# Dilated attention by residues modulo 4 in place of parities: 320 keys a query in place of 416, fp32 products on small array tiles

## The chip, the cores and the metric

The kernel runs on one core of a Trainium2 chip. A core has a matrix engine (TensorE, PE in the profile; its weight loads are listed as PEld), a vector engine (VectorE, DVE), a scalar engine (ScalarE, ACT), GpSimd (POOL) and SyncE (SP), which here only issues transfers. TensorE writes into PSUM, eight banks of 512 fp32 columns on 128 partitions. The metric is the device time of one execution in microseconds (us).

## The reference

One encoder layer on a stream of 512 positions and 1024 channels, fp32 throughout. A combined input projection gives the recurrent input, a gate, and q, k, v. The recurrent half is a gated linear recurrence in both directions. The other half is what the change touches: attention with 8 heads of 64 channels, with three windows for each query and a bias by relative position. Both halves are normed and go through an output projection of 1024 x 1024, and a two-layer MLP (1024 to 4096 to 1024) follows.

```python
DILATED_PATTERNS = ((128, 1), (512, 4), (2048, 16))
for window, dil in DILATED_PATTERNS:
    half = window // (2 * dil)
    offs = jnp.arange(-half, half + 1, dtype=jnp.int32) * dil
...
    logits = einsum(q, k[kpos]) * scale + bias        # NEG_INF where kpos is outside 0..S-1
    lse = logsumexp(logits); p = exp(logits - lse); outs.append(einsum(p, v[kpos]))
w = softmax(stack(lses))
o = sum(w * stack(outs))
```

So a query at position i needs every key with |j - i| up to 64, every fourth key (same residue modulo 4) with |j - i| up to 256, and every sixteenth key anywhere. A key that lies in two or three windows counts two or three times. Combining the windows by their denominators is the same as one softmax over all keys with the logarithm of that count added to the bias, and both kernels compute it so: one table of biases by relative position, with a large negative number where no window reaches.

## The kernel before, in words

**Stages.** The input projection comes first, in the order recurrent input, gate, v, then q and k for the first pair of heads. The attention stage follows, from about 94 to 176 us of the profiled execution. Then come the rest of the output projection, the MLP in two halves, and the final norm. Large products are made from splits: an operand is written as a rounded high part (ScalarE, line 247 for weights) and the remainder (VectorE, line 269), and a product is three matmuls (`mm3`, lines 312 to 314). The gates of the recurrence (`lru_gates`, PSUM name `pg`, line 528) are plain fp32 on tiles of 64 x 64 of the array. A plain fp32 matmul leaves two records in the trace.

**Attention before.** Heads go in four pairs p, one head of a pair on partitions 0 to 63 and the other on 64 to 127. Keys and queries are ordered by parity: even positions, then odd ones. For every pair there are four query tiles of 128, numbered u in the loop.

- `att_s` (line 806): scores, 128 queries x 416 keys, as three split products for each of two heads; a call makes two query tiles, so 12 matmuls. The 416 keys are the 256 of the query's own parity and 160 near ones of the other parity.
- `att_e`: VectorE adds the biases and finds the minimum (line 822); ScalarE takes the exponential and sums it (line 823).
- `att_t` (line 842): TensorE turns the weights in 128 x 128 blocks, six for each (p, u), into `pt`; ScalarE copies them out (line 845). `att_c` (line 851) turns the remaining 32 columns on VectorE.
- `att_av` (line 942): values, 24 matmuls of 64 output rows for a pair, plain fp32, the operand `vs` stationary. VectorE multiplies by the reciprocals of the sums (line 948), which come through a small round trip to DRAM (`att_z`, `att_zd`).
- `load_tw` (lines 476 and 478): biases for a head and a key offset, two transfers each from the table `nbd` in DRAM, 32 in all.
- `q_evac`, `k_evac`, `s_hi`, `s_lo` (lines 778, 784, 788): q and k are taken from PSUM, then split in a high and a low part; the first 256 columns of k are repeated behind the others by a transfer.

**The order around it.** The loop at lines 1139 to 1176 runs i = 0 to 4, u = 0 to 3. Step (i, u) issues the scores of pair i and the transposes of pair i - 1, and between them `fill` takes projection steps off a list: first the q and k projections of the later pairs, then the first half of the output projection (`wo_thunks`). The table `plan` puts the recurrence's leftovers and the splits at fixed places. Each engine works its own instructions in the order written out here. SP's transfers are in a fixed order too: weights, biases, and the round trip. PSUM is divided into four banks for projections (`pj`), two for scores and values (`gs`) and two for transposes (`et`). A weight block is read from DRAM (`wraw`), split (`whi`, `wlo`), and lasts for eight projection steps.

## Time and profile before

| what | value |
|---|---|
| median of 3 runs | 525.96 us (525.91 to 526.02) |
| span of the profiled execution | 524.0 us |
| TensorE busy | 517.3 us, 99% of the span, 3021 records |
| VectorE busy | 430.3 us, 82% |
| ScalarE busy | 351.9 us, 67% |
| chain that ended last | 96% TensorE |

The span runs from the first instruction to the last in one profiled execution; the time of a run also holds what lies around it. The views used below are: the page's totals of each engine; the chain of work that ended last, followed back from the last instruction; groups of instructions by line (busy time, mean and extremes of one in ns, when the first started and the last ended); and stretches, which give each engine's busy time in a window. A line such as `PE ps L806 x12` is twelve TensorE records that write to `ps`, issued by line 806 of the kernel.

### The profile page before, as it was taken

How to read it: one execution, taken by the hardware profiler on the slowest of the kernel's cores; microseconds unless marked ns; L12 is line 12 of the kernel's file. 1: busy time of each engine (PE TensorE's matmuls, PEld its weight loads, DVE VectorE, ACT ScalarE, POOL GpSimd, SP SyncE). 2: the span in 40 equal slices, each digit the busy share in tenths (PEclk: the TensorE clock that was granted, in tenths of full speed). 3: DMA queues.
4: the chain of work that ended last, by engine and by line, in shares of the span. 5: the costliest groups of instructions: out<-in, count | busy, mean ns of one | idle time of the engine just before them, and what ended most of it. 6: DMA issues, size and time to landing. Idle time of an engine off the chain costs nothing.

```text
span 524.0 us, 8211 instructions
## 1 busy us (share of the span) xinstructions
PE 517.3 (99%) x3021; PEld 444.0 (85%) x3021; DVE 430.3 (82%) x668; ACT 351.9 (67%) x568; POOL 65.8 (13%) x90
## 2 busy tenths in 40 slices
PE   9999999999999999999999999999999999999995
PEld 8867888778787788899999888889999999888884
DVE  6899986788886898898789987789766978986985
ACT  7579946667855848585578666565667577655664
POOL 0173000000000321001300311001101300140000
PEclk9999999999999999999999999999999999999999
DMA  8636545367696499847595899976977497799804
GB/s 288 213 98 198 160 155 180 91 182 206 185 286 218 102 194 275 326 129 196 136 225 144 217 273 275 309 268 161 295 235 194 116 226 208 154 286 256 201 1 161
DMA packets 40329, 105.15 MB, mean 201 GB/s; under 512 B 5056, under 2 KB 13376, under 8 KB 40288
## 3 DMA queue, kind: packets, MB, share of 16 engines
q1 hardware_dynamic: 32448, 78.10, 44.7%
q0 software_dynamic: 7696, 26.32, 27.1%
q8 instruction: 24, 0.39, 0.3%
q10 hardware_dynamic: 144, 0.20, 0.1%
q14 instruction: 17, 0.14, 0.1%
HBM read 95.59 MB, written 4.29 MB: 191 GB/s over the span
## 4 chain that ended last, share of the span: by engine, by line
PE 96%; issue 2%; DVE 1%; POOL 1%; DVEq 0%; ACT 0%; POOLq 0%; ACTq 0%
PE pu L313 10%; PE pu L312 10%; PE pu L314 10%; PE pd L312 10%; PE pd L313 10%; PE pd L314 10%; PE pqk L312 3%; PE pqk L314 3%; PE pqk L313 3%; PE pwo L312 2%; PE pt L842 2%; PE pwo L314 2%; PE pwo L313 2%; PE ps L806 2%; PE pav L942 2%
## 5 line engine op out<-in xcount | busy, mean ns | idle before, releaser
L269 DVE TENSOR_TENSOR wlo<-wraw,whi 128x1024 fp32r<-128x1024 f32 x71 | 86.6, 1221 | 23.1 <-ACT whi L247 22.9
L247 ACT ACTIVATE whi<-wraw 128x1024 fp32r<-128x1024 f32 x67 | 70.8, 1058 | 37.5 <-PE pd L314 18.2
L313 PE MATMUL pd<-wlo,ah 128*128 128x512 f32 (+1 forms) x195 | 75.2, 386 | 0.0
L312 PE MATMUL pd<-whi,ah 128*128 128x512 f32 (+1 forms) x195 | 75.2, 386 | 0.0
L314 PE MATMUL pd<-whi,al 128*128 128x512 f32 (+1 forms) x195 | 75.2, 386 | 0.0
L314 PE MATMUL pu<-hh,wlo 128*128 128x256 f32 x224 | 63.4, 283 | 0.0
L313 PE MATMUL pu<-hl,whi 128*128 128x256 f32 x224 | 63.4, 283 | 0.0
L312 PE MATMUL pu<-hh,whi 128*128 128x256 f32 x224 | 63.4, 283 | 0.0
L269 DVE TENSOR_TENSOR wlo<-tw,whi 128x1024 fp32r<-128x1024 f32 x37 | 45.2, 1221 | 18.1 <-ACT whi L247 18.1
L312 PE MATMUL pu<-h2h,whi 128*128 128x256 f32 (+1 forms) x200 | 60.1, 300 | 0.0
L313 PE MATMUL pu<-h2l,whi 128*128 128x256 f32 (+1 forms) x200 | 60.0, 300 | 0.0
L314 PE MATMUL pu<-h2h,wlo 128*128 128x256 f32 (+1 forms) x200 | 60.0, 300 | 0.0
L247 ACT ACTIVATE whi<-tw 128x1024 fp32r<-128x1024 f32 x38 | 40.1, 1059 | 26.3 <-PE pd L314 6.3
L247 ACT ACTIVATE whi<-ts 128x1024 fp32r<-128x1024 f32 x24 | 25.5, 1061 | 26.3 <-PE pd L314 18.3
L312 PEld LDWEIGHTS pu<-hh,whi 128*128 128x128 f32 x224 | 43.0, 192 | 0.0
L313 PEld LDWEIGHTS pu<-hl,whi 128*128 128x128 f32 x224 | 43.0, 192 | 0.0
L314 PEld LDWEIGHTS pu<-hh,wlo 128*128 128x128 f32 x224 | 43.0, 192 | 0.0
L314 PEld LDWEIGHTS pd<-whi,al 128*128 128x128 f32 x195 | 36.6, 188 | 7.4
L312 PEld LDWEIGHTS pd<-whi,ah 128*128 128x128 f32 x195 | 36.6, 188 | 7.3
L313 PEld LDWEIGHTS pd<-wlo,ah 128*128 128x128 f32 x195 | 36.6, 188 | 7.3
L312 PEld LDWEIGHTS pu<-h2h,whi 128*128 128x128 f32 x200 | 38.3, 191 | 1.3
L314 PEld LDWEIGHTS pu<-h2h,wlo 128*128 128x128 f32 x200 | 38.3, 191 | 1.3
(277 smaller groups left out, 1219.8 us busy)
## 6 DMA issues: line engine op xcount, KB each, us to landing
wraw<-in_w_up_dram SPq DMA_DIRECT2D x25, 512.0 KB, 4.4
ts<-in_w_dn_dram POOLq DMA_DIRECT2D x24, 512.0 KB, 13.3
wraw<-in_w_dn_dram SPq DMA_DIRECT2D x24, 512.0 KB, 9.2
tw<-in_w_up_dram SPq DMA_DIRECT2D x15, 512.0 KB, 5.1
tw<-in_w_up_dram POOLq DMA_DIRECT2D x15, 512.0 KB, 8.3
wraw<-in_w_in_dram SPq DMA_DIRECT2D x13, 512.0 KB, 3.8
ts<-in_w_dn_dram SPq DMA_DIRECT2D x8, 512.0 KB, 6.8
tw<-in_w_dn_dram SPq DMA_DIRECT2D x8, 512.0 KB, 7.3
```

Source lines behind the costliest of these rows:

```text
L247: act(hi, raws[i], AF.Copy)
L269: nc.vector.tensor_tensor(lo, r, f(splits[i][0]), op=OP.subtract)
L312: nc.tensor.matmul(o, lhsT=a[0], rhs=b[0], start=bool(first), stop=False, skip_group_check=on)
L313: nc.tensor.matmul(o, lhsT=a[0], rhs=b[1], start=False, stop=False, skip_group_check=on)
L314: nc.tensor.matmul(o, lhsT=a[1], rhs=b[0], start=False, stop=bool(last), skip_group_check=on)
L806: nc.tensor.matmul(psq[p, u][e][:, :NK], lhsT=qs_[p, a][r, P * qt:P * qt + P], rhs=kks[p][r, b, w:w + NK], start=i == 0, stop=i == 2)
L842: nc.tensor.transpose(pt[:, i * P:(i + 1) * P], en[h][qt][:, k:k + P], ident)
L942: nc.tensor.matmul(pav[p][a, co], lhsT=vs[:, jt, h * DH:(h + 1) * DH], rhs=et[h, jt][:, ci], start=jt == 0 and i == 0, stop=jt == 3 and i ...
```

## The change

Positions are kept in natural order in k, and reversed in q, and a step of the attention takes all 128 queries of one residue c modulo 4. They fall in four groups g of 32 queries, each group spread over 128 positions. A group reads 256 consecutive keys around it (near), and 64 keys of the same residue from the rest of the sequence in steps of four (far): 320 keys. The 64 x 32 tiles of the array hold four groups by two heads, eight products side by side.

- Scores (`att_s`) are plain fp32, one product in place of three. There are 8 near ones of 256 columns and 8 far ones of 64 for each (pair, residue); q and k are no longer split (`s_hi`, `s_lo` go), and k's first 192 columns are repeated by a ScalarE copy (`k_wrap`).
- The weights of a residue are turned by VectorE in blocks of 32 x 32 (`att_t`: one instruction over 128 x 320 for each head and residue). The TensorE transposes, their copies and `att_c` go.
- Values (`att_v`) use tiles of 32 x 64, four groups by two heads, into four banks: 64 near matmuls of 128 columns and 64 far ones of 32 columns for a pair. Each group needs its own keys on its own 32 partitions, so the values are written to DRAM (`vd`, six transfers) and read back in four layouts (`load_v4`, eight transfers from POOL for each pair).
- The result leaves the four banks by four VectorE multiplies (`att_o`) in place of one.
- A head's biases (`load_tw`) are ten transfers in place of four; `fill` issues two of them, or of the value loads, with each projection step (`side`).
- Scores and values share the banks `gs` and `et`. In loop step (i, 0) stand the scores of residues 0 and 1, in (i, 1) the near values of pair i - 1 and the transposes of residues 0 and 1, in (i, 2) the far values and their multiplies, in (i, 3) the scores of residues 2 and 3, whose transposes stand in (i + 1, 0). The last pair's values move from behind the loop into round i = 4.
- Some operands of the input projection and of the MLP share buffers with the turned weights (`slot`, `keep`, tag `g5`); the pool of general tiles shrinks from 45 to 33.

```diff
-WN = 160
-NK = TH + WN
+NW = 2 * P
+NFAR = 64
+NK = NW + NFAR
+WLO = (TH, 192, 64, 0)
+WFAR = (0, 448, 320, 256)
-    NG = 45
+    NG = 33
...
+    def load_tw(h):
+        def near(g):
+            nc.sync.dma_start(at_(t, 32 * g * ps, (ps, 32), (NK, 4), (1, NW)), at_(nbd, b + P * g + WLO[g], (4, 32), (1, 4), (1, NW)))
+        def far(g, y0, y1, o):
+            nc.sync.dma_start(at_(t, 32 * g * ps + NW + y0, (ps, 32), (NK, 4), (1, n)), at_(nbd, b + 2 * S + o + y0, (1, 32), (0, 4), (1, n)))
+        return [lambda g=g: near(g) for g in range(4)] + [lambda a=a: far(*a) for a in FARS]
+    def load_v4(p):
+        def near(g):
+            nc.gpsimd.dma_start(t[32 * g:32 * g + 32, :8, :], at_(vd, (NV * p + WLO[g]) * P, (P, 32), (32 * P, 8), (1, P)))
+        def far(g):
+            nc.gpsimd.dma_start(t[32 * g:32 * g + 32, 8:, :], at_(vd, (NV * p + WFAR[g]) * P, (4 * P, 32), (P * P, 2), (1, 4 * P)))
...
     def q_evac(p, pp):
-        t = raw[p, 0] = g_("qraw")
-        stt(t[:, ::-1], pp, -(DH ** -0.5), rstd, op0=OP.mult, op1=OP.mult)
+        t = qs_[p] = g_("q")
+        stt(at_(t, S - 1, t.ap[0], (-1, 2), (-2, TH)), by_parity(pp), -(DH ** -0.5), by_parity(rstd), op0=OP.mult, op1=OP.mult)
     def k_evac(p, pp):
+        nc.vector.tensor_tensor(in_turn(t[:, :S]), by_parity(pp), by_parity(rstd), op=OP.mult)
+        wraps.append(lambda: act(t[:, S:], t[:, :192], AF.Copy))
-    def s_hi(p, is_k): ...
-    def s_lo(p, is_k): ...
...
-    def att_s(p, us):
-                    nc.tensor.matmul(psq[p, u][e][:, :NK], lhsT=qs_[p, a][r, P * qt:P * qt + P], rhs=kks[p][r, b, w:w + NK], start=i == 0, stop=i == 2)
+    def att_s(p, cs):
+        for c in cs:
+            b = psq[p, c] = [ps_("ps", "et" if c % 2 else "gs") for _ in range(2)]
+            def each(c0, n, rhs):
+                for g in range(4):
+                    r0 = 3 - c + P * g
+                    for e, r in enumerate(halves):
+                        nc.tensor.matmul(b[e][32 * g:32 * g + 32, c0:c0 + n], lhsT=qs_[p][r, r0:r0 + 125:4], rhs=rhs(kks[p][r], g),
+                                         start=True, stop=True, skip_group_check=True)
+            each(0, NW, lambda k, g: k[:, WLO[g]:WLO[g] + NW])
+            each(NW, NFAR, lambda k, g: k[:, WFAR[g] + c:WFAR[g] + c + 253:4])
...
-    def att_t(h, jt):
-            nc.tensor.transpose(pt[:, i * P:(i + 1) * P], en[h][qt][:, k:k + P], ident)
-        act(t[:, c], pt[:, c], AF.Copy)
-    def att_c(h, jt):
-        nc.vector.transpose(et[h, jt][:, c], en[h][qt][:, c])
+    def att_t(p, c):
+        for e in range(2):
+            nc.vector.transpose(et[p][:, 2 * c + e, :], en.pop((2 * p + e, c)))
-    def att_av(p, jts): ...
+    def att_v(p, far):
+        def each(blk, c0, n, col, dims, first=False, last=False):
+            for g in range(4):
+                for e in range(2):
+                    nc.tensor.matmul(o[g][64 * e:64 * e + 64, c0:c0 + n], lhsT=v[32 * g:32 * g + 32, blk, 64 * e:64 * e + 64],
+                                     rhs=at_(t, 32 * g * ps + e * NK + col, (ps, 32), *dims), start=first, stop=last, skip_group_check=True)
+        if not far:
+            for k in range(8):
+                each(k, 0, P, 32 * k, ((2 * NK, 4), (1, 32)), k == 0)
+        else:
+            for c in range(4):
+                for f in range(2):
+                    each(8 + 4 * f + c, 32 * c, 32, 2 * c * NK + NW + 32 * f, ((1, 32),), last=f == 1)
+    def att_o(p):
+        for g in range(4):
+            nc.vector.tensor_tensor(at_(y, 254 - 64 * g, ...), at_(o[g], 0, ...), at_(z, 32 * g, ...), op=OP.mult)
...
     def fill(n):
+            if len(wraps) > 1 or wraps and not late_wrap:
+                k_wrap()
+            late_wrap[:] = [1] if wraps and not late_wrap else []
+            for _ in range(2):
+                if side:
+                    side.popleft()()
...
-                    if u % 2 == 0:
-                        att_s(i, (u, u + 1))
+                if i < 4 and u in (0, 3):
+                    att_s(i, (0, 1) if u == 0 else (2, 3))
+                if i and u in (1, 2):
+                    att_v(i - 1, u == 2)
+                if i and u == 0:
+                    att_t(i - 1, 2)
+                    att_t(i - 1, 3)
+                    att_z(i - 1)
+                if i < 4 and u in (0, 3):
+                    att_e(i, 0 if u == 0 else 2)
+                    att_e(i, 1 if u == 0 else 3)
+                if i < 4 and u == 1:
+                    att_t(i, 0)
+                    att_t(i, 1)
+                if i and u == 2:
+                    att_o(i - 1)
...
-    att_av(3, range(4))
```

## The prediction

> **What bounds the kernel now.** I read the page's engine totals first, then the chain that ended last, then that chain in order of time, then the stretches of the attention stage.

> ```profile
> span 524.0 us, 8211 instructions
> ...
> PE 517.3 (99%) x3021; PEld 444.0 (85%) x3021; DVE 430.3 (82%) x668; ACT 351.9 (67%) x568; POOL 65.8 (13%) x90
> ...
> PE 96%; issue 2%; DVE 1%; POOL 1%; DVEq 0%; ACT 0%; POOLq 0%; ACTq 0%
> ```

> TensorE is the chain: 96% of it. So an edit is worth what it does to TensorE's own stream, unless another engine falls behind. Attention's share of that stream stands in the chain in order of time (start, length, what):

> ```profile
> 33.74 7.03 PE pg L528 x64
> ...
> 94.07 1.33 PE ps L806 x12
> 95.40 0.43 PE pqk L312
> 95.82 0.23 PE pqk L313
> ...
> 109.44 0.80 PE pt L842 x6
> ...
> 112.98 0.66 PE pt L842 x6
> ...
> 133.00 2.96 PE pav L942 x24
> ...
> 159.49 5.76 PE pav L942 x48
> ```

> ```profile
> L806 PE MATMUL ps<-kk,qh x64: 341/348/457, 94.0 to 151.8; 64*128 64x416 f32 x64
> L806 PE MATMUL ps<-kk,ql x32: 341/348/350, 94.9 to 152.2; 64*128 64x416 f32 x32
> ...
> L842 PE MATMUL pt<-ident,e x96: 270/272/329, 109.4 to 169.9; 128*128 128x128 f32 x96
> ...
> L942 PE MATMUL pav<-ett,vs x96: 299/379/563, 132.9 to 174.0; 128*64 128x416 f32 x32, 128*64 128x256 f32 x32, 128*64 128x160 f32 x32
> ```

> Scores (ps): 96 records are 8 groups of 12. A group lasts 1.33 us and makes the matmul behind it last 0.43 in place of 0.23, so it costs 1.53 us: 12.2 us in all. Transposes (pt): 16 groups of 6 at 0.66 us, 10.5 us (a group behind ps shows 0.80, but then takes over the 0.20). Values (pav): four head pairs at 2.96 us, 11.8, and 0.2 where a projection follows. **Together 34.7 us of TensorE**, from 94 to 176 us. Everything between these groups stays as it is.

> **What is removed, added and moved.**

> *TensorE, by columns.* The pg row prices plain fp32 on small tiles: the 32 products of the gates are 64 records, four at once (two row halves, two column halves), so 16 rounds of 512 columns in 7.03 us: 0.44 us a round, 0.86 ns a column and pass, two passes to a product. The pav row agrees: for each head 1664 columns in two passes are 2.86 us of the 2.96. That leaves 0.10 us at the group's front, and with the 0.20 behind it 0.30 us for changing the array over.

> With all tiles running at once, eight of them here, the new groups need at least:
> - scores, two residues: 2 x 2 x (256+64) x 0.86 ns = 1.10, with changeover 1.40 us; 8 groups, 11.2 us;
> - values near: 8 blocks x 2 x 128 x 0.86 ns = 1.76, with changeover 2.06; 4 groups, 8.2 us;
> - values far: 8 x 2 x 32 x 0.86 ns = 0.44, with changeover 0.74; 4 groups, 3.0 us.

> That is 22.4 us, **12.3 us less than now**, with no transposes left on TensorE.

> *TensorE, by instructions.* The columns get fewer, the instructions do not. Each product is two records, each with its weight load. Scores: 16 (pair, residue) x 16 products x 2 = 512. Values: 4 x 128 x 2 = 1024. So 1536 pairs of load and matmul take the place of 288, and TensorE's records go from 3021 to 4269. A scores group has 64 pairs in 1.10 us, or 17 ns a pair; the far values have 128 pairs in 0.44 us, 3.4 ns a pair. Nothing in this trace is fed at such a rate: the pg group has 110 ns a record, pav 123 ns. What the feed can do shows at one place only, where two waits of TensorE's sequencer stand close together:

> ```profile
> L942 PEldq EVENT_SEMAPHORE  x2: 51/51/51, 171.5 to 171.7; - x2
> ```

> Unrounded they start at 171.538 and 171.663 us. In program order two weight loads and two matmuls of pav lie between them. So 125 ns less the first wait's 51 are 74 ns for four instructions, at most 18.5 ns each. Elsewhere such a wait starts some 20 ns after the queue gives a place to the instruction ahead of it; if the second wait cost that too, 13.5 ns are left. A pair then costs 27 to 37 ns of feeding. As a floor, four pg loads that had been queued start 7 ns apart, so a queued burst is much faster than the feed. Counted in the same trace, the sequencer stands 16 pairs ahead where nothing holds it, so 16 pairs of each group go at burst speed.

> From below the feed may cost nothing beyond the columns (-12.3 us). From above, 37 ns a pair. I take 31, between the two readings of the only row that bears on it:
> - scores: 48 x 31 ns = 1.49, with changeover 1.79; 8 groups, 14.3 us;
> - values, near and far alike: 112 x 31 ns = 3.47, with changeover 3.77; 8 groups, 30.2 us.

> 44.5 us, or **9.8 us more than now**. At 27 ns it is 39.4 us (+4.7); at 37 it is 52.2 us (+17.5).

> [...]

> Strided operands have no row: the far keys and the weights of the scores are read in steps of four elements. From nothing (hidden under the feed) to four times as long: the far passes of the scores would then be 0.22 us in place of 0.055, 32 of them, +5.3 us. I take nothing, since a matmul fed every 31 ns has 0.25 us until its tile comes round again, and keep the other end.

> *VectorE.*

> ```profile
> L822 DVE CUSTOM_DVE_ANT_0 e<-ps,tw 128x416 f32<-128x416 f32 x32 | 17.5, 586 | 4.3 <-PE ps L806 4.3
> ...
> L851 DVE STREAM_TRANSPOSE ett<-e 128x32 f32<-128x32 f32 x32 | 4.8, 188 | 0.0
> ...
> L784 DVE TENSOR_TENSOR kk<-kraw,kk 128x512 fp32r<-128x512 f32 x4 | 2.7, 670 | 0.7 <-ACT kk L778 0.7
> ...
> L440 DVE STREAM_TRANSPOSE cst<-ysq 128x512 f32<-128x512 f32 x2 | 1.4, 708 | 0.0
> ```

> Between 188 ns (32 columns) and 708 (512) a transpose of 320 comes to 0.50 us: 32 of them, +16.0, against 32 x 0.188 = 6.0 removed. The reduction loses 96 of 416 columns, about 0.10 us, 32 times: -3.2. Eight splits of q and k at 0.67 go: -5.4. One multiply of 0.69 per pair becomes four of 128 columns, some 0.28 each: +1.7. Net +3.1 us. ScalarE only loses work (the splits, the copies of pt).

> ```profile
> 94.00:109.00 15.00, 15.00 (x83) 11.90 (x84) 12.13 (x27) 9.57 (x22) 0.00 (x0) 1.00 0.50 140
> 109.00:125.00 16.00, 16.00 (x94) 12.80 (x92) 12.53 (x37) 12.75 (x31) 0.00 (x0) 1.00 0.63 186
> 125.00:141.00 16.00, 16.00 (x105) 12.20 (x102) 14.50 (x40) 11.98 (x28) 1.04 (x1) 1.00 0.63 160
> 141.00:158.00 17.00, 17.00 (x102) 13.76 (x101) 13.78 (x40) 11.40 (x32) 0.00 (x0) 1.00 0.94 289
> 158.00:176.00 18.00, 18.00 (x125) 12.39 (x124) 13.90 (x31) 11.72 (x25) 0.00 (x0) 1.00 0.54 184
> ```

> The columns are PE, PEld, DVE, ACT, POOL, clock, DMA share. VectorE has 66.8 us of these 82; with 69.9 in a stage that gets longer it stays covered. [...]

> *Banks and the tail.* Scores and values now share the same four banks in turn, so the near values wait for the last score reductions (four at 0.57 us with the accumulator read). Three or four projection steps of 0.68 us and the longer groups cover that. In the last round they hardly do: behind the last scores come four reductions, then ScalarE's last exponents (0.75 us each, with the read), then two transposes of 0.50, and only then the values. From the first residue's scores at half of the group that is about 0.9 + 2.3 + 1.4 + 1.0 = 5.6 us, against 1.8 for the group and 3.4 for the five steps between; the splits of weights that stand between on both engines (1.06 and 1.22 us) lengthen it. **+1.0 us** (0 to 3), which TensorE cannot fill, as the values stand ahead of the steps behind them. The last pair's values stand some steps earlier than before, so the norm behind them is late for nobody.

> *DMA.*

> ```profile
> L476 SPq DMA_DIRECT2D tw<-nbd x12: 319/448/467, 102.8 to 145.0; - x12
> L478 SPq DMA_DIRECT2D tw<-nbd x12: 424/429/433, 103.3 to 145.5; - x12
> ```

> A head's biases are ten issues in place of four: 80 at 0.44 us, 35 us of SP in place of 14. The worst place is step 20, where twenty stand together: 9 us in front of the next weights. One block of weights lasts eight steps, 5.4 us, and three loaded plus three split ones lie ahead: covered; without them it would be late by 9 - 5.4 us once. Six writes of the values and 32 loads from POOL (idle here, by the rows above) have two score groups before their reader. I count nothing.

> **The sum.** 524.0 + 9.8 + 1.0 = 534.8 us of span. The median, 525.96, lies 1.96 above the span, so 537 us. With the feed at 27 to 37 ns and the tail at 0 to 3: 531 to 547.

> **Rivals.** 0.2%, about 1 us, is what a measurement here tells from nothing.

> 1. [...] Chance 0.31.
> 2. *The feed lies at break-even*, 22 ns a pair: scores 1.36 x 8, values 2.76 x 8, 33 us, -1.7 + 1.0: 525. Chance 0.07.
> 3. *Feeding and strides add*: the far scores read at a quarter of the rate on top of 37 ns: about 550. The strides have no row for or against. Chance 0.07.
> 4. *SP's queue late*: ScalarE's wait for raw weights appears in front of whi, up to 4 us on top of the forecast, 541. Inside the forecast's range; the three blocks ahead speak against it.

> **Numbers.** My forecast, the feed at 27 to 37 ns, has 0.55 with what rival 4 adds; 537, own range 531 to 546. Slower: 0.55 + 0.07 = 0.62. Faster 0.31, within 0.2% 0.07. The range reaches down to rival 1: 516 to 547.

> **What would show it.** Fed by the sequencer, the near and far values last the same, some 3.5 us each, though their columns are 4 to 1; by columns they last 1.8 and 0.5. A scores group lasts 1.5 or more against 1.1. VectorE's transposes should be near 0.50 us. If TensorE shows idle time in front of the values in rounds 1 to 3, VectorE or the banks bind, not the feed. I am wrong if the far values come out near 1 us.

## The result and the profile after

The changed kernel takes **572.39 us** (median of 4 runs, 571.58 to 574.78) against 525.99 before: a ratio of 1.089 (95% interval 1.0868 to 1.0913). The forecast was 537 (516 to 547). The direction was right, the size was not: 46 us in place of 11.

The page of the changed kernel, first the totals, the chain and the queue of program fetches:

```profile
span 569.8 us, 10806 instructions
...
PE 533.1 (94%) x4269; PEld 457.2 (80%) x4269; DVE 433.5 (76%) x672; ACT 333.8 (59%) x532; POOL 83.6 (15%) x122
...
q8 instruction: 33, 0.54, 0.4%
...
PE 82%; issue 7%; DVE 5%; DMA 4%; ACT 1%; POOL 1%; SPq 0%; DVEq 0%; POOLq 0%; ACTq 0%
```

TensorE's records are the 4269 that were counted, and VectorE's 433.5 us are 3.2 more than before, as worked out (+3.1). But TensorE is no longer the chain: its share of the span falls from 99% to 94%. It stands idle, and it stands idle in the places that the view of its waits names (what it waited for; us in all, times, longest):

```profile
PE pav L860 <- issue: 8.7, 4, 4.3
PE pav L860 <- DVE mn L839: 8.2, 3, 5.1
PE ps L825 <- issue: 5.1, 2, 3.7
PE pu L326 <- DVE a L1396: 3.6, 1, 3.6
PE pwo L326 <- DVE x L1214: 3.4, 1, 3.4
```

That is 29.0 us; before, the only such row was 0.8 us at the start, which the changed kernel has too. The second loss follows most of these waits: the granted clock falls to 0.50 in seven stretches (an eighth, at the end of the span, is in the kernel before as well). The first of the seven and the sum of all (columns: length, busy time of TensorE, its loads, VectorE, ScalarE, POOL, then the clock, DMA share, GB/s):

```profile
117.70:124.50 6.80, 6.64 (x132) 5.37 (x133) 6.48 (x16) 3.91 (x10) 0.00 (x0) 0.50 0.65 70
...
sum 37.40, PE 34.01 PEld 28.81 DVE 26.15 ACT 13.63 POOL 6.20; mean PE 4.86 PEld 4.12 DVE 3.74 ACT 1.95 POOL 0.89
```

Behind each of the seven waits of 2.9 us and more (2.9 to 5.1) the clock was granted at one half here, for 3.4 or 6.8 us; behind the two shorter ones (1.4 us at 186.71, 0.8 us at 203.3) it was not. A projection matmul takes 0.43 us in these stretches and 0.23 outside them. TensorE is busy for 34.0 us in the seven; taken at half the rate, which is an estimate, 17.0 us are lost. Idle and half clock together are **46 us, the whole of the difference** of the spans (569.8 less 524.0). TensorE's own stream, taken at full clock, costs about what it did (533.1 less 17.0, against 517.3).

**Where the idle time lies.** The chain in order of time, cut to what is not a projection step:

```profile
100.94 11.48 DMA wraw<-in_w_in_dram
112.50 1.06 ACT whi L261
...
118.51 4.50 PE pav L860 x124
...
137.22 3.69 issue
140.91 0.42 PE ps L825 x2
...
148.79 4.25 issue
...
164.20 9.82 DMA ws<-in_w_out_dram
...
186.71 1.42 issue
```

There are four kinds.

*Weights and inputs that come late*: 5.1 us ahead of the values at 112.5, 2.9 us at 171.7. A block of weights issued at 100.94 took 11.48 us to land, behind it stand the split, the transposes on VectorE and the values. SP's own order in time shows why it was issued so late; first before, then after:

```profile
81.80 7.23 SPq L230 DMA_DIRECT2D wraw<-in_w_in_dram  x3
92.14 0.67 SPq L785 DMA_DIRECT2D kk<-kk  x1
```

```profile
87.66 0.73 SPq L244 DMA_DIRECT2D wraw<-in_w_in_dram  x1
88.44 0.65 SPq L497 DMA_DIRECT2D tw<-nbd  x1
89.15 2.95 SPq L502 DMA_DIRECT2D tw<-nbd  x6
93.31 2.64 SPq L497 DMA_DIRECT2D tw<-nbd  x4
96.00 4.84 SPq L502 DMA_DIRECT2D tw<-nbd  x4
100.94 1.46 SPq L244 DMA_DIRECT2D wraw<-in_w_in_dram  x1
```

Fifteen issues for biases stand between two weight blocks, and they get slower towards the end (four far ones take 4.84 us, where the median of one is 0.43). And the DMA engines are far busier: the stretch ahead of the attention, first before, then after (the last but one column is the DMA share), and the packets on the two pages.

```profile
76.00:94.00 18.00, 18.00 (x81) 14.64 (x79) 12.07 (x13) 11.60 (x15) 0.00 (x0) 1.00 0.48 157
...
DMA packets 40329, 105.15 MB, mean 201 GB/s; under 512 B 5056, under 2 KB 13376, under 8 KB 40288
```

```profile
76.00:93.40 17.40, 17.40 (x78) 14.14 (x76) 10.13 (x11) 10.81 (x14) 2.38 (x5) 1.00 0.84 222
...
DMA packets 48577, 109.38 MB, mean 192 GB/s; under 512 B 12512, under 2 KB 20592, under 8 KB 48528
```

The share rises from 0.48 to 0.84, the packets under 512 B from 5056 to 12512.

*Program fetches*: stalls in the middle of a group, where no semaphore is waited for (137.22, 148.79, 186.71, and 0.8 us at 203.3; 10.1 us in all). A packet of the instruction queue is 16 KB: the 9 packets more (33 against 24) serve 2496 loads and matmuls more, some 280 each. Counted in TensorE's own order, waits included, the four stalls lie 256, 1280 and 512 instructions apart, all multiples of 256: they are at the edges of fetched blocks. In each of the long ones a packet of that queue arrives; the view of the transfers between 137.2 and 140.9 us:

```profile
q8 instruction: 1, 0.02, 1.7%
```

The packet lands at 139.5, and TensorE goes on at 140.9; in all four stalls it goes on 1.2 to 1.4 us after the landing. In the kernel before, each block has landed 12 us or more before its first instruction runs; in the attention of the changed kernel 9 us at best, and at the four stalls between 0.3 us ahead and 3.2 us after TensorE has come to its edge.

*The last round*: 3.4 us ahead of the last pair's values (192.4) and 3.4 us ahead of the second half of the output projection (214.5). The chain ahead of the values:

```profile
190.51 0.96 ACT whi L261
...
192.64 0.74 DVE x L984
193.38 1.13 DVE tw L1070
194.51 1.22 DVE ett L849 x3
```

*The MLP*: 3.6 us at 462.9, in a part of the kernel that the change does not touch but for its buffers.

### The profile page after: what moved, and what is told of

Read it like the earlier page. It is cut to its first block, busy times and chain, and to the rows that moved or that the text cites. A ratio compares the mean times of both kernels' runs of the same rounds, so it can differ in the third digit from the quotient of the medians.

```text
span 569.8 us, 10806 instructions
## 1 busy us (share of the span) xinstructions
PE 533.1 (94%) x4269; PEld 457.2 (80%) x4269; DVE 433.5 (76%) x672; ACT 333.8 (59%) x532; POOL 83.6 (15%) x122
## 2 busy tenths in 40 slices
DMA packets 48577, 109.38 MB, mean 192 GB/s; under 512 B 12512, under 2 KB 20592, under 8 KB 48528
## 4 chain that ended last, share of the span: by engine, by line
PE 82%; issue 7%; DVE 5%; DMA 4%; ACT 1%; POOL 1%; SPq 0%; DVEq 0%; POOLq 0%; ACTq 0%
PE pu L326 9%; PE pd L327 9%; PE pd L328 9%; PE pd L326 9%; PE pu L327 9%; PE pu L328 9%; PE pav L860 3%; PE pqk L326 2%; PE pqk L327 2%; DMA wraw<-in_w_in_dram 2%; PE pqk L328 2%; DMA ws<-in_w_out_dram 2%; PE pwo L326 2%; PE pwo L328 1%; PE pwo L327 1%
## 5 line engine op out<-in xcount | busy, mean ns | idle before, releaser
L326 PE MATMUL pu<-h2h,whi 128*128 128x256 f32 (+1 forms) x200 | 61.3, 306 | 3.6 <-DVE a L1396 3.6
L327 PEld LDWEIGHTS pu<-h2l,whi 128*128 128x128 f32 x200 | 39.4, 197 | 1.3
L328 PEld LDWEIGHTS pu<-h2h,wlo 128*128 128x128 f32 x200 | 39.4, 197 | 1.3
```

The lines of the kernel that those rows point to most:

```text
L326: nc.tensor.matmul(o, lhsT=a[0], rhs=b[0], start=bool(first), stop=False, skip_group_check=on)
L327: nc.tensor.matmul(o, lhsT=a[0], rhs=b[1], start=False, stop=False, skip_group_check=on)
L328: nc.tensor.matmul(o, lhsT=a[1], rhs=b[0], start=False, stop=bool(last), skip_group_check=on)
```

## The experiments

The theory after this reading (T): late transfers set the stage's pace, and late program fetches are a consequence of the same traffic. The rival (D): 256 instructions used up in 2 to 3 us outrun the fetch whatever the traffic is.

**1. Fewer transfers, the same program on TensorE.**

```diff
     def load_tw(h):
+        if h > 1:
+            tws[h] = twb[h % 2]
+            return []
     def load_v4(p):
+        if p:
+            v4[p] = v4b[0]
+            return []
```

The first two lines alone:

> The changed kernel with the biases of the first two heads loaded once and used for all heads: 60 of the 80 bias transfers are left out, so six heads get wrong biases. TensorE's instructions are the same. Theory T (transfers): the weights come late because SP issues the biases ahead of them and because the DMA engines are busy, and the program fetches of TensorE come late for the same reason. Then the idle 5.1 us ahead of the values at 112.5 and the 2.9 us at 171.7 go, the stalls in the middle of a group (3.7, 4.3, 1.4, 0.8 us) shrink to half or less, the half-clock stretches behind them go, and the time falls by 20 to 27 us, to 545 to 552. Rival D (density): TensorE uses up 256 instructions in 2 to 3 us in these groups, faster than any fetch comes. Then the stalls inside the groups stay at about 10 us and only the 8 us of late weights go with some 5 us of half clock: 558 to 562.

Measured: 543.60 us, 1.0325 (1.0293 to 1.0357), a little more gain than theory T's range.

The second alone:

> The changed kernel with the values of the first pair of heads read from DRAM once and used for all four pairs: 24 of the 32 value transfers from POOL are left out, so three pairs get wrong values. The biases are as in the changed kernel. Theory T, DMA engines as the cause: packets of POOL are 15% of the engines' time in the stage, so late weights and late fetches shrink by a third or more: 555 to 562. Theory T, SP's order as the cause: SP issues what it did, weights as late as before: 569 to 573. Rival D: stalls inside groups unchanged, 568 to 573.

Measured: 557.68 us, 1.0621 (1.0584 to 1.0658).

Both:

> Both of these together: biases of two heads and values of one pair loaded once, 84 transfers left out, outputs wrong for the other heads; TensorE's program is the same. Theory T: no late weights, no fetch stall inside a group; what stays is the round behind the loop and the wait in the MLP (3.4 + 3.4 + 3.6 us idle with 6 us of half clock): 538 to 546. Rival D: fetch stalls stay at some 10 us with their half clock, 553 to 560.

Measured: 543.04 us, 1.0333 (1.0317 to 1.0349). The waits that are left in this kernel, and one stretch of its attention:

```profile
PE pu L326 <- DVE a L1407: 3.6, 1, 3.6
PE pav L871 <- DVE ett L860: 3.6, 1, 3.6
PE pwo L326 <- DVE x L1225: 3.5, 1, 3.5
PE pav L871 <- issue: 1.5, 2, 1.2
PE ps L836 <- issue: 1.1, 1, 1.1
```

```profile
125.00:141.00 16.00, 16.00 (x363) 12.37 (x361) 14.40 (x38) 7.45 (x19) 1.05 (x1) 1.00 0.23 59
```

With the same instructions and fewer transfers the late weights are gone and the fetch stalls fall from 10.1 to 2.6 us. From 94 to 158 us TensorE has no idle time. So **the transfers decide**, and the biases are the larger part of them. Whether it is by SP's issues or by the traffic, the runs without biases don't tell, since they lack both. The density is not innocent: the stalls that remain are in dense groups too, where a block is used up before a fetch is there. In the second run SP issues all that it did, and 14.7 us go: of the two readings the one by the DMA engines holds, at least for these.

**2. The same transfers, fewer products.**

```diff
-            for k in range(8):
+            for k in range(1):
                 each(k, 0, P, 32 * k, ...)
-                for f in range(2):
+                for f in (1,):
                     each(8 + 4 * f + c, ...)
```

> The changed kernel with all its transfers, but with one of eight blocks of the near values and half of the far ones: 24 of 128... that is 40 records of a near and far group in place of 256, the output is wrong. The instructions of TensorE fall by 1728 of 8538. Rival D: with the dense groups mostly gone no stall inside a group is left: 15 us of value groups, 10 us of stalls and their half clock go, late weights stay: 535 to 542. Theory T: the values' own time goes (some 13 us) and the stalls in value groups (5 us and 3 us of clock), the waits for late weights and the stalls in score groups stay: 546 to 554.

(The text miscounts: 80 of 256 records of a pair's values are left, and 1408 instructions go.) Measured: 560.67 us, 1.0673 (1.0623 to 1.0723). Both theories missed. 1408 instructions less bring 12 us, because other waits take the room:

```profile
PE pav L860 <- DVE mn L839: 18.7, 5, 9.2
PE pwo L326 <- DVE x L1214: 6.0, 1, 6.0
PE pav L860 <- issue: 3.9, 1, 3.9
```

The last row is the wait ahead of the last pair's values (183.6), not a fetch. No fetch is late any more: every block has landed 4.2 us or more before its first instruction, though all transfers are there. So a late fetch takes both, the dense products and the traffic; on this point the rival was half right. But TensorE waits 18.7 us for banks that VectorE frees late, whose own inputs are late (VectorE stands 5.4 us for biases ahead of 141.9, and 8.9 us for `x` ahead of 166.3): with all transfers in place the stage does not go much faster, however little TensorE has to do.

**3. SP's order or the engines' traffic.** All 80 bias transfers are issued by POOL:

```diff
-            nc.sync.dma_start(at_(t, 32 * g * ps, ...
+            nc.gpsimd.dma_start(at_(t, 32 * g * ps, ...
```

> The changed kernel with all 80 bias transfers issued by POOL in place of SP; the same bytes and packets, nothing left out. If SP's order is what makes the weights late (80 issues in front of them, 51 us of SP in the changed kernel), the weights come on time and the time falls towards that of the kernel with 20 bias transfers (543.6): 546 to 556. If it is the traffic on the DMA engines (fetches and weights wait behind the biases' small packets, whoever issues them), it stays at 565 to 575.

Measured: 560.97 us, 1.0673 (1.0655 to 1.0690), between the two. With SP free 11.4 us go, and the longest fetch stall is even longer (5.4 us). The bytes are the same, but the packets are not, against what the expectation says: issued by POOL, the biases go in fewer and larger ones (48577 packets and 109.38 MB in the changed kernel):

```profile
DMA packets 40130, 109.39 MB, mean 195 GB/s; under 512 B 6368, under 2 KB 10864, under 8 KB 40080
```

The engines stay as busy (a share of 0.96 from 94 to 109 us, 0.99 in the changed kernel), and POOL's loads of the values now stand behind its biases. So the 11.4 us are no clean price of SP's order. The counter-test leaves SP's 80 issues and cuts the traffic: each bias is loaded once into a staging tile, in 259-wide rows from which POOL copies the four shifted windows.

```diff
-            nc.sync.dma_start(at_(t, 32 * g * ps, (ps, 32), (NK, 4), (1, NW)),
-                              at_(nbd, b + P * g + WLO[g], (4, 32), (1, 4), (1, NW)))
+            nc.sync.dma_start(at_(sg, 32 * g * ps, (ps, 32), (1, NW + 3)),
+                              at_(nbd, b + P * g + WLO[g], (4, 32), (1, NW + 3)))
+            nc.gpsimd.tensor_copy(at_(t, c0, (pt_, P), (NK, 4), (1, n)), at_(sg, o, (ps, P), (step, 4), (1, n)))
```

> The changed kernel with each bias loaded once into a staging tile (a row of 259 for the four shifted windows of 256, and the far biases once in place of four times); POOL copies them out to the four residues with two copies a head. Nothing is left out. SP still issues 80 bias transfers, but they hold a quarter of the bytes and of the packets (320 a head in place of 1280). If traffic is what makes weights and fetches late: 545 to 553. If SP's order is: 565 to 575. If neither quite, in between.

Measured: 550.61 us, 1.0482 (1.0450 to 1.0514), as the traffic theory had it: 21.8 us go. It is no clean price either, since SP's 80 issues take 38 us here in place of 51. The two gains, 11.4 and 21.8, come to more than the 28.8 of the run without the biases, so they overlap. But both runs have nearly the same number of packets (40130 and 40899), and the one with 3.9 MB less to move (105.48) is 10.4 us faster: the number of packets alone does not set the loss.

**4. The MLP's wait.** Two general tiles more, in the kernel with both loaded once:

```diff
-    NG = 33
+    NG = 35
...
-        t = tws[h] = twb[h] = work.tile([P, 4 * NK], FT, name="tw", tag="tw", bufs=4)
+        t = tws[h] = twb[h] = work.tile([P, 1024], FT, name="tw", tag="tw", bufs=4)
...
```

> The kernel with biases of two heads and values of one pair loaded once, with the biases of one residue used for all four as well (the bias tile shrinks from 1280 to 1024 columns); the space holds 35 general tiles in place of 33. Outputs are wrong. If the wait of 3.6 us in the MLP is one for a free general tile, it goes, with the 3.0 us of half clock behind it: 536 to 537.5 against 543.0. If it comes from the order of work on ScalarE and VectorE, it stays: 542 to 544.

Measured: 535.64 us, 1.0193 (1.0177 to 1.0209), 7.4 less than without: 3.6 of wait, 3.0 of half clock behind it, and some 1 us because another half-clock stretch, behind the norm's wait, lasts 3.4 us in this profile in place of 6.8. The row of line 1407 is gone from the waits (one of 1.2 us for late fetches is left out):

```profile
PE pav L871 <- DVE ett L860: 3.6, 1, 3.6
PE pwo L326 <- DVE x L1225: 3.5, 1, 3.5
...
PE ps L836 <- issue: 1.0, 1, 1.0
```

The pool that the change cut from 45 tiles to 33 (and 10 places in the shared ones) is too small for the MLP by two tiles at most: ScalarE waits for a free tile until TensorE has read an old one (6.0 us, until 462.1 in the changed kernel), VectorE stands behind ScalarE, and TensorE behind VectorE.

**5. The last round.** Three projection steps moved in front of the last pair's values:

```diff
-    FILL = {(3, 0): (1, 1, 1, 0), (3, 1): (1, 1, 1, 0), (3, 2): (1, 1, 1, 0), (4, 0): (0, 1, 0, 0),
+    FILL = {(3, 0): (1, 1, 0, 0), (3, 1): (1, 1, 0, 0), (3, 2): (1, 1, 0, 0), (4, 0): (1, 1, 1, 1),
```

> The kernel with biases of two heads and values of one pair loaded once (543.0), with three projection steps moved from behind the first three steps of round 3 to the first step of round 4, so that seven or eight steps stand between the last scores and the last pair's values in place of five. If the wait of 3.6 us in front of these values is the chain reduction, exponent, transpose that five steps can't cover, it falls by about 2 us and its half clock (1.6) goes: 539 to 541. If the sum of work behind the last scores decides, the wait only moves to the norm behind the values: 542.5 to 544.

Measured: 536.16 us, 1.0214 (1.0187 to 1.0241), 6.9 less than without and more than expected: the whole wait of 3.6 us ahead of the values is gone, with its half clock (1.6). The wait for the norm behind them (3.5 us) stays as it was, but the half clock behind it is the shorter one here too.

**6. Do the causes add up?** All edits of experiments 1 (both), 4 and 5 together:

> All causes that were found taken away together, with wrong outputs: biases of two heads and one residue and values of one pair loaded once, 35 general tiles, three projection steps moved. If the causes add up, 543.0 less 7.4 less 6.9: 527.5 to 530. What then still stands above the kernel before is the wait for the norm behind the values (3.5 us with 1.7 of half clock) and 1 to 2 us of late fetches; TensorE's attention groups should sum to some 30 us against 34.7 before.

Measured: 530.26 us, 1.0096 (1.0067 to 1.0125), just above the range; the sum by the single runs is 528.8, and the half clock behind the norm lasts 6.8 us again. And a version with the whole computation: staged biases for both heads of a pair in one transfer (40 issues), the moved steps, and three buffers that attention no longer needs reused in the MLP (the staging tile takes the place of one general tile, so 32 are left):

```diff
+            nc.sync.dma_start(at_(sg, 32 * g * ps, (ps, 32), (W, 2), (1, NW + 3)),
+                              at_(nbd, b + P * g + WLO[g], (4, 32), (NBD, 2), (1, NW + 3)))
...
+            if n == "22":
+                opa[n, p] = keep(6 + p) if p > 1 else work.tile([P, NV], FT, name="as", tag="kk", bufs=2)[:, :S]
+            elif n == "s3" and p == 1:
+                opa[n, p] = work.tile([P, 2 * 324], FT, name="as", tag="stage", bufs=1)[:, :S]
```

> A version with the whole computation: the changed kernel with the biases of both heads of a pair staged in one go (40 bias transfers from SP in place of 80, a quarter of the packets, four POOL copies a pair), three projection steps moved in front of the last pair's values, and three buffers that attention no longer needs (two of k, the staging tile) used for MLP operands. If the causes add up: 550.6 for staging alone, less 7 for the MLP's wait with its half clock, less 7 for the tail, less 4 to 6 for the inputs that SP issued late behind the biases: 531 to 536. If they overlap, so that one wait takes another's place: 538 to 546.

Measured: 530.62 us (527.73 to 534.92), 1.0107 (1.0055 to 1.0159). The causes add up, and 42 of the 46 us are regained. In its profiled execution (527.73 us, the fastest of the four) the clock stays at 1.00 until the end, and one wait of more than 0.8 us is left:

```profile
PE pwo L326 <- DVE x L1223: 3.4, 1, 3.4
```

**7. That last wait.** I took the norm's place in VectorE's order for its cause and put it ahead of a weight split and two sums, then between them:

```diff
     fill(1)
+    att_y(3)
+    rc[1] = rstd_cols(col_sums(ssy[1]), S)
     conv_lo(C_WA + 2)
...
-    att_y(3)
-    rc[1] = rstd_cols(col_sums(ssy[1]), S)
```

> The combined version with the sum of squares and the norm of attention's half put directly behind the last values, ahead of a weight split (1.22 us of VectorE) and two operand sums, in place of behind them. Nothing is left out. In the combined version TensorE stands 3.4 us in front of the second half of the output projection until this norm is there (at 182.7 us; its last square was ready at 174.4). If the norm's place in VectorE's order is the cause, the wait goes by 2.5 us or more: 3 us below the combined version, 524.5 to 528.5. If the split that now comes later takes its place, no change against the combined version.

Measured: 531.75 us, the median of five executions (a sixth took 539.14); 1.0129 (1.0107 to 1.0150).

> The same with the norm behind the weight split but ahead of the two operand sums. Half of the way: the norm comes some 1.5 to 2 us earlier than in the combined version and no split is late; 525.5 to 529 if the split matters to the version with the norm first, else 1 us above it.

Measured: 531.27 us, 1.0105 (1.0081 to 1.0130). The gain did not come: the wait is still 2.8 us in either profile, and neither time can be told from the combined version's. In the chain of the version with the norm first, the split that was passed now stands at the end, as that run's second reading had it:

```profile
181.97 0.17 DVE rv L428
182.14 1.13 DVE wlo L283
183.27 0.66 DVE x L993
```

That speaks for the sum of VectorE's work behind the last values, and against its order, but no run took work away there, so it is not shown. No version here is faster than the kernel before.

## Why the prediction was wrong

**"I count nothing" for the DMA is the step that failed.** I looked at the place with twenty bias issues together, put it at 9 us of SP and found three blocks of weights ahead. The issues stood elsewhere too (88 to 101 us) and took 51 us of SP in all, not 35, and weights issued among the biases' packets were slow themselves (11.48 us to land). Rival 4 named the place, SP's queue, and allowed it 4 us on top. With 84 transfers left out (experiment 1) 29 us go. I had worked out the number of issues but not that of packets and bytes; with a quarter of the biases' and the same 80 issues (staging), 22 us go.

**The feed was mis-sized.** I took 31 ns for a pair of load and matmul, from two waits of the sequencer, and expected 9.8 us more for the groups. The groups without idle time at full clock stand in the kernel with both loaded once (chain in order of time):

```profile
103.50 1.58 PE ps L836 x63
...
112.58 2.02 PE pav L871 x125
...
117.55 1.42 PE pav L871 x91
...
131.07 2.80 PE pav L871 x125
```

With the 0.20 us behind each: scores 1.78 (forecast 1.79, by columns 1.40), near values 2.22 (forecast 3.77, by columns 2.06), far values 1.62 (forecast 3.77, by columns 0.74). The far values have 128 pairs in 1.42 us, 11 ns a pair. So these near values come out close to their columns and the far ones well above theirs, as by a cost of each pair, at a third of the price I took; whether the feed or the array sets it is not shown. 8 x 1.78 + 4 x 2.22 + 4 x 1.62 = 29.6 us, **5.1 less than the 34.7 before**. That is the best case: the near values of the next pair take 2.80 us (131.07), at full clock and without a wait in sight, for a reason that stays open. Over the whole span TensorE's busy time at full clock is 3.8 us below the kernel before (520.9 less half of the 14.8 at half clock, against 517.3). So TensorE's part came out on the side of a feed that costs little beyond the columns, though not with the 12.3 us less that columns alone would give, and the sign that I named against me (far values near 1 us, not 3.5) came out nearer to 1. The lower end of the range, 516, and the chance of 0.31 for a faster kernel were my estimate for that side; no run shows the 12.3 us, and the groups at full clock show 5.1 in their place. In the changed kernel itself half clock hides this: the same near values take 4.50 us at 118.5. The scores' agreement is no proof of the feed: their second and third rounds start 0.22 us apart (93.69 and 93.90 in the changed kernel), which is 256 columns at 0.86 ns.

**The tail** was put at 1.0 us (0 to 3) and is 6.8 of idle time in two waits. The chain of reduction, exponent and transpose was right; that VectorE has other work (an addition of 0.74 and a weight sum of 1.13 us by the rows above, and a split) in front of the transposes was not counted in full, and "the norm behind them is late for nobody" was wrong.

**Not seen at all**: that the pool of general tiles, cut from 45 to 33, would be missed in the MLP (3.6 us and half clock behind it; the diff showed the number); that the program itself comes by transfer, in blocks of 256 instructions, and can be late (no stall in the kernel before, 4.25 us at 148.79 here); and that the granted clock falls to 0.50 behind a wait, seven times here, which turns 29 us into 46.

**Right**: 4269 records; VectorE's transposes at 0.48 us (0.50 forecast), its reductions 0.10 us shorter, its multiplies at 0.28, and the net of +3.1 us. The groups by line:

```profile
L839 DVE CUSTOM_DVE_ANT_0 e<-ps,tw 128x320 f32<-128x320 f32 x32 | 14.1, 488 | 13.1 <-PE ps L825 6.7 <-DMA tw<-nbd 5.6 <-issue 0.6
L849 DVE STREAM_TRANSPOSE ett<-e 128x320 f32<-128x320 f32 x32 | 13.5, 478 | 0.0
...
L875 DVE TENSOR_TENSOR yp<-pav,zrow 128x128 f32<-128x128 f32 x16 | 3.5, 284 | 15.6 <-PE pav L860 15.6
```

So the right sign was luck: the forecast had 9.8 us from a feed that costs nothing of the kind, and nothing from the transfers that cost 29 of the 46.

What stays open: how the loss divides between SP's order, the number of small packets and the bytes, since both runs of experiment 3 changed more than one of them; and why a fetch in the attention can start 7 to 10 us after TensorE has entered the block before it (7.4 us at 138.5 and 9.7 us at 150.6 in the changed kernel) while the engines' mean share is not full all that time (8.7 us even in the kernel with both loaded once). The trace does not say which engine carries a packet, and this wasn't tried.

## What to carry to other kernels

Count a change's transfers in packets and bytes as well as in issues, and look at what else uses the same engines, weights and the program itself; a stage whose engine is 99% busy has no room for a late block. Price a wait of TensorE at more than its length where the profile shows the clock fall behind it: here 29 us of idle time cost 46. And when a diff cuts a shared pool of buffers, look at the last place that uses it, however far from the change.
